# Attention's q and k loads written a component at a time, delta-rule loads counted later, new order weights

## The chip, the cores and the metric

The kernel is one launch on one core of a Trainium2 chip. The metric is device time in microseconds (us), the median of several runs. Five engines work on the core, each through its own stream of instructions in order: TensorE (PE), VectorE (DVE), ScalarE (ACT), GpSimd (POOL) and SyncE (SP). SP computes nothing. It issues the transfers between memory (DRAM) and the on-chip buffers, which have 128 partitions, and 16 DMA engines carry them out.

## What is computed

One layer over 1024 latent tokens and 256 context tokens, 1024 wide, in float32. A combined projection feeds two branches: a bidirectional gated delta rule (8 heads, a scan over chunks) and differential attention (8 heads, two softmaxes of 64 dimensions each per head). Both are normalised, gated, projected, merged and mapped by an output projection. Cut to what matters here:

```python
t = rms_norm(raw.reshape(b, length, DIFF_HEADS, 2, DIFF_DQK), gain)   # q and k: 8 heads, 2 components of 64
...
s = jnp.einsum('bqhcd,bkhcd->bhcqk', qi, k).astype(jnp.float32) * scale
p = jax.nn.softmax(s, axis=-1)
attn = p[:, :, 0] - lam * p[:, :, 1]
return jnp.einsum('bhqk,bkhv->bqhv', attn.astype(v.dtype), v)
...
s_next = s * jnp.exp(gl_i)[..., None, None] + jnp.einsum('bhck,bhcv->bhkv', kd_i, v_new)
```

## The kernel before, in words

Float32 products are made from rounded high parts and low remainders. For a product of weights and activations that means three matmuls in place of one. In attention's scores the two halves of the partitions hold the high and the low part of k, and the matmul sums over both; q's high part `qh` stands in both halves, and q's low part `ql` likewise.

The program runs in stages: front and convolution; the projections of attention's q, k and v; the delta rule; attention; merge and output. The delta rule's scans (`scan`, one for each direction) go head by head over ten chunks, and PE's pauses between their steps are filled with the projections' matmuls (`mm`, out of `fill_flow`). At a change of head, `sets` loads the head's v, k (twice) and q (`vv`, `kk`, `sk`, `sq`), and `loads` loads one pair of chunks at a time (`x`).

Attention (`scores`, `soft`, `turns`, `att_out` and others) goes through 64 tiles: 8 heads of 8 tiles, 128 queries each. A tile takes 12 score matmuls (`s`, two components, three pieces of keys, `qh` then `ql`), an evacuation on DVE, the exponential on ACT, ten transposes (`t`) and, for two tiles together, 30 matmuls with v (`v`). The merge's matmuls (`ma`, from weights `wq` and values `y`) fill PE between them.

`att_load_ops(h)` loads `qh` and `kk` of head h, four transfers. `att_low_ops(h)` loads `ql`, two transfers. Two heads' tiles are held at a time, so the loads of head h wait for the last score of head h-2 (`seen_`). Before, each transfer fills 64 partitions: 64 lines of the 128 of a component-by-dimension array are read in an order that puts component 0 and component 1 of a dimension beside each other. The tiles `vh` and `vl` of v (`att_values`) and the gate `sz` (`gates_in`) have one buffer, and are loaded when the head before has finished with them.

All of attention's loads go through SP's one queue, in the order that the planner wrote down. That order of all engines is made before the chip sees anything. Each stream of work yields steps with an engine, an assumed duration and what they depend on; the planner keeps a clock for each engine and always takes the step that can start first (`flow` in the delta rule, `turn_flow` elsewhere, where steps within `TOL` of one another go by their stream's bias). `ABIAS` holds attention's biases; a stream's bias grows with the tile it works on (`due`). `later(t, us)` makes a result count as ready that much later in the planner's clock. It changes the order alone and puts no wait into the program.

Of the kernel before, what the change touches and what calls it, by code (L numbers as in the profile page):

```python
# [8 lines left out]
F32 = mybir.dt.float32  # L9
# [11 lines left out]
L = 1024  # L21
# [13 lines left out]
PE, DVE, ACT, POOL, DMA, ADMA, DV2, PL1 = range(8)  # L35
# [8 lines left out]
class Block:  # L44
# [193 lines left out]
    def front(self, st, early, kv0):  # L238
# [190 lines left out]
        for g, b in ((loads(), 0), (modulation(), 1), (smalls(), 1), (rms(), 2), (weights(), 1.5), (turns(), 1), (self.forever(turnq[0]), 1.2),  # L429
                     (self.forever(turnq[1]), 1.2), (main(), 9)):  # L430
            self.stream(g, b)
# [822 lines left out]
    def sets(self):  # L1254

        nc = self.nc
        free = []
        for h in range(H):
            yield lambda: self.gs and min(self.scanned) >= h and self.tailed >= h - 1
            w = dict(seen={}, oa=self.gs.tile([P, NL, P], F32, tag=f"oa{h % 2}", name="oa"))  # L1260
            free = [self.over, self.ready[h - 1]["tail"] if h else None]
            for n, src in (("vv", self.gv[h]), ("kk", self.gkk[h]), ("sk", self.gkq[h][:, :LT]), ("sq", self.gkq[h][:, LT:])):
                if h == 0 and n == "kk":
                    yield lambda: all((d, 0, 8) in self.units_ for d in range(2))
                w[n] = self.gs.tile([P, L] if n == "sq" else [P, NT, P] if n in ("kk", "vv") else [P, LT], F32, tag=n, name=n)
                w["t" + n] = yield DMA, 1.82, free, lambda: nc.sync.dma_start(
                    w[n], src.rearrange("(c p) f -> p c f", p=P) if n in ("kk", "vv") else src)
            self.ready[h] = w

    def loads(self, d):  # L1270

        nc, i = self.nc, 0
        order = ((8, 0, 2, 4, 6), (8, 6, 4, 2, 0))[d]
        for h in range(H):
            for c in order:
                yield lambda: self.gs and self.stored > h and len(self.used_[d]) > i - 2
                x, e = self.gs.tile([P, 2, 2, P], F32, tag=f"x{d}", name="x", bufs=2), 2 if c < NL else 1
                u = dict(x=x[:, 0], qk=x[:, 1])
                u["tx"] = yield DMA, 0.45 * e, [self.store_t[h], self.used_[d][i - 2] if i > 1 else None], \
                    lambda: nc.sync.dma_start(x[:, :e], self.xq[h][:, d, c // 2, :e])  # L1280
                if c < NL:
                    u["tqk"] = yield POOL, 0.72, [self.later(u["tx"], 1.0)], lambda: nc.gpsimd.tensor_tensor(
                        x[:, 1], x[:, 1], (self.up, self.lo)[d].unsqueeze(1).to_broadcast([P, 2, P]), ALU.mult)
                self.units_[d, h, c] = u
                i += 1
# [145 lines left out]
    def named(self, n, gen):  # L1431
        s = self.entry[n] = [gen, self.ABIAS.get(n, 0), None, None]
        s[2] = next(gen, None)
        self.streams.append(s)

    def due(self, n, i):

        self.entry[n][1] = self.ABIAS.get(n, 0) + self.DUE * i

# [48 lines left out]
    def att_load_ops(self, h):  # L1488

        q, pool, tags = self.nc.sync, self.a0 if h % 2 else self.gh[0], ("qh", "kk") if h % 2 else ("kq", "X")  # L1490
        w = self.aT[h] = dict(qh=pool.tile([P, 2, L], F32R, tag=tags[0], name="qh"),
                              kk=pool.tile([P, 2, LT], F32R, tag=tags[1], name="kk"))
        old = self.seen_.get(h - 2)
        w["t"] = []
        for s in range(2):
            d, v = slice(64 * s, 64 * s + 64), lambda x: x.rearrange("(c d) n -> d c n", c=2)
            w["t"] += [(yield DMA, 1.46, [old], lambda: q.dma_start(w["qh"][d].bitcast(F32), v(self.qd[0, h]))),
                       (yield DMA, 1.82, [old], lambda: q.dma_start(w["kk"][d].bitcast(F32), v(self.kd[s, h])))]

    def att_low_ops(self, h):  # L1500

        w = self.aT[h]
        w["ql"] = self.a0.tile([P, 2, L], F32R, tag=f"ql{h % 2}", name="ql")
        w["tl"] = []
        for s in range(2):
            w["tl"].append((yield DMA, 1.46, [self.seen_.get(h - 2)], lambda: self.nc.sync.dma_start(
                w["ql"][64 * s:64 * s + 64].bitcast(F32), self.qd[1, h].rearrange("(c d) n -> d c n", c=2))))

    def att_heads(self):
        for h in range(H):  # L1510
# [219 lines left out]
    def side_start(self):  # L1730
# [10 lines left out]
    ONACT = (1, 2, 3)  # L1741
    TOL = 0.02
    PACE = 4.48
    ABIAS = dict(rels=-0.59, softs=8.84, norms=5.82, gateq=-27.29, sums=-14.54,
                 outs=-42.85, lows=-2.4, highs=-9.33, adds=26.02, scales=31.0, evs=22.29, mouts=-3.31,
                 att_out=8.18, turns=3.19, scores=-12.11, merge=1.0)
    KEEP = 3

    def side_values(self):
# [453 lines left out]
```

## Time and profile before

| what | us |
|---|---|
| median of three runs (1963.87 to 1965.93) | 1964.13 |
| the profiled execution, its own time | 1966.57 |
| its span, first to last instruction | 1964.8 |
| PE busy in the span | 1909.4 |
| first score matmul of attention | 1297.4 |
| first score matmul of head 7 | 1720.3 |

The profile's page gives busy time by engine, 40 slices of the span, DMA queues, the chain of work that ended last, and groups of instructions. Other answers of the trace give one tile's instructions, who waited for whom, an engine's instructions in order of time, and busy time, DMA share and rate in chosen stretches. A DMA share of 1 means that all 16 DMA engines were busy; a little over 1 comes from packets that overlap. The PE column counts matmul ends that are modelled, so a full PE is not necessarily at its peak.

### The profile page before, as it was taken

The page shows a single profiled execution, that of the slowest core. Times are in us where ns is not written, and L with a number is a line of the kernel's source. Part 1 is how long each engine was busy: PE and PEld are TensorE (multiplying, and loading weights), DVE is VectorE, ACT ScalarE, POOL GpSimd, SP SyncE. Part 2 cuts the span into 40 slices and gives each one's busy share as a digit, 9 for nine tenths or more (in the row PEclk, how much of TensorE's full clock was granted, in tenths as well). Part 3 has the DMA queues.
Part 4 walks back from the last instruction along what each step waited for, and adds up shares of the span by engine and source line. Part 5 has one row for each costly group of instructions (what it writes and reads, how often), then busy time and mean ns, then how long its engine had stood idle before and what let it go on. Part 6 is the DMA issues. An engine that isn't in the chain of part 4 may idle for free.

```text
span 1964.8 us, 37491 instructions
## 1 busy us (share of the span) xinstructions
PE 1909.4 (97%) x13807; PEld 1679.4 (85%) x13807; DVE 1465.1 (75%) x3613; ACT 1069.4 (54%) x2191; POOL 677.4 (34%) x610
## 2 busy tenths in 40 slices
PE   6999999999999999999999999999999999999999
PEld 4988888899999998888888888877888888888887
DVE  4687998948877987778777673336688979895677
ACT  4543445335325464767755745456687868884222
POOL 3200000005431332343433234233666757762203
PEclk9999999999999999999999999999999999999999
DMA  9144544674546557866777466585566684426542
GB/s 329 60 132 107 144 94 114 145 220 140 183 132 211 150 191 207 257 208 211 249 217 248 114 221 214 153 202 159 159 161 151 156 230 132 129 87 209 182 155 86
DMA packets 383038, 336.39 MB, mean 171 GB/s; under 512 B 142609, under 2 KB 323443, under 8 KB 381831
## 3 DMA queue, kind: packets, MB, share of 16 engines
q1 hardware_dynamic: 382855, 333.99, 57.4%
q8 instruction: 109, 1.79, 0.4%
q14 instruction: 74, 0.61, 0.1%
HBM read 222.14 MB, written 111.79 MB: 170 GB/s over the span
## 4 chain that ended last, share of the span: by engine, by line
PE 77%; DVE 8%; DMA 7%; ACT 3%; issue 2%; SPq 1%; POOL 1%; DVEq 0%; ACTq 0%; POOLq 0%
PE mm L56 38%; PE s L56 6%; PE v L56 6%; PE chain L56 5%; PE mb L56 5%; PE ma L56 4%; PE x L56 3%; PE t L63 3%; PE out L56 2%; DVE S L1560 1%; PE gram L56 1%; DMA vv<-gv 1%; DVE ac L595 1%; PE pz L56 1%; DMA g<-gt 1%
## 5 line engine op out<-in xcount | busy, mean ns | idle before, releaser
L56 PE MATMUL mm<-hs,wh 128*128 128x512 f32 (+1 forms) x2048 | 648.2, 390 | 1.5 <-DVE hs L408 1.4
L56 PEld LDWEIGHTS mm<-hs,wh 128*128 128x128 f32 x2048 | 371.9, 190 | 60.8 <-issue 2.7
L56 PE MATMUL mm<-hs,wl 128*128 128x512 f32 (+1 forms) x1024 | 398.4, 389 | 1.1 <-issue 1.1
L56 PE MATMUL mm<-wh,hs 128*128 128x256 f32 (+1 forms) x1792 | 332.7, 286 | 0.3 <-ACT sq L977 0.3
L56 PEld LDWEIGHTS mm<-wh,hs 128*128 128x128 f32 x1792 | 280.7, 191 | 0.8 <-ACT sq L977 0.5
L1560 DVE TENSOR_SCALAR_CACHE_REDUCE S<-s,rsq 128x512 f32<-128x512 f32 (+1 forms) x384 | 241.4, 656 | 29.4 <-PE s L56 25.9
L56 PE MATMUL mm<-wl,hs 128*128 128x256 f32 (+1 forms) x896 | 255.6, 285 | 0.0
L56 PEld LDWEIGHTS mm<-hs,wl 128*128 128x128 f32 x1024 | 194.4, 190 | 28.7 <-issue 0.9
L1597 POOL TENSOR_TENSOR S<-S 128x1280 f32<-128x1280 f32 x64 | 188.6, 2954 | 78.0 <-ACT S L1590 77.1
L1573 ACT ACTIVATE S<-S,mn 128x1280 f32<-128x1280 f32 x128 | 175.3, 1371 | 44.9 <-DVE mn L1572 43.2
L56 PEld LDWEIGHTS mm<-wl,hs 128*128 128x128 f32 x896 | 171.3, 191 | 0.1
L595 DVE SCALAR_TENSOR_TENSOR ac<-xc,convT,ac 128x1284 f32<-128x1284 f32 (+1 forms) x96 | 138.8, 1449 | 11.9 <-ACT ac L593 11.2
L56 PE MATMUL s<-kk,qh 128*128 128x512 f32 (+1 forms) x384 | 144.5, 376 | 2.9 <-DVE S L1560 2.9
L56 PE MATMUL s<-kk,ql 128*128 128x512 f32 (+1 forms) x384 | 134.0, 359 | 2.5 <-DMA ql<-qd 2.5
L1634 DVE TENSOR_TENSOR al<-t,ah 128x512 fp32r<-128x512 f32 (+1 forms) x192 | 109.5, 596 | 29.8 <-ACT ah L1629 28.9
L1629 ACT CAST ah<-t 128x512 fp32r<-128x512 f32 (+1 forms) x192 | 91.9, 518 | 32.6 <-PE t L63 15.3
L580 POOL MEMSET xc<- 128x2 f32 (+1 forms) x64 | 3.6, 101 | 297.8 <-ACT sq L629 113.6
L63 PE MATMUL t<-ct,S 128*128 128x128 f32 x640 | 98.6, 277 | 4.1 <-DVE al L1634 2.6
L1157 DVE TENSOR_TENSOR ts<-ts,tmp 80x31 f32<-80x31 f32 (+15 forms) x248 | 97.5, 393 | 6.1
L1318 ACT ACTIVATE vd<-chain,edk 128x128 f32<-128x128 f32 x144 | 52.3, 370 | 89.2 <-PE chain L56 83.7
L1155 DVE TENSOR_TENSOR tmp<-ab,ts 80x31 f32<-80x31 f32 (+15 forms) x248 | 94.5, 381 | 8.5 <-DMA ab<-da 3.0
L56 PE MATMUL v<-ah,vh 128*128 128x256 f32 x320 | 93.0, 291 | 0.0
(296 smaller groups left out, 4338.3 us busy)
## 6 DMA issues: line engine op xcount, KB each, us to landing
wr<-in_w_in_dram SPq DMA_DIRECT2D x48, 512.0 KB, 6.0
hx<-in_w_in_dram SPq DMA_DIRECT2D x64, 256.0 KB, 6.4
x<-xq SPq DMA_DIRECT2D x64, 256.0 KB, 3.8
X<-gcd SPq DMA_DIRECT2D x8, 1280.0 KB, 8.3
kd<-col SPq DMA_DIRECT2D x40, 256.0 KB, 2.2
xq<-X SPq DMA_DIRECT2D x16, 640.0 KB, 7.4
kk<-kd SPq DMA_DIRECT2D x16, 640.0 KB, 7.9
kq<-gkq SPq DMA_DIRECT2D x8, 1152.0 KB
```

The lines of the kernel that those rows point to most:

```text
L56: self.nc.tensor.matmul(out, lhsT, rhs, start=start, stop=stop)
L63: self.nc.tensor.transpose(out, src, self.ident[:src.shape[0], :src.shape[0]])
L580: x["e"].append((yield PL1, 0.1, [old], lambda: nc.gpsimd.memset(xc[:, a:b], 0.0)))
L595: t = yield DV2, 1.21e-3 * wd, [t], lambda: nc.vector.scalar_tensor_tensor(ac[:, :wd], xc[:, j:j + wd], self.convw(j, x["ct"]), ac[:, :wd] ...
L1155: t = yield DV2, n * w / 960.0 + 0.08, [t if j else self.later(t, 2.5), t1], lambda: V.tensor_tensor(tv, ab[:, j + 1:, j:j + 1].to_broadca ...
L1157: t = yield DV2, n * w / 960.0 + 0.08, [t, t1], lambda: V.tensor_tensor(ts[:, j + 1:, :w], ts[:, j + 1:, :w], tv, ALU.subtract)
L1318: td = yield ACT, 0.251, [t], lambda: nc.scalar.activation(vd, pc[:, 1], AF.Copy, scale=self.edk[:, c, g:g + 1])
L1560: e = yield DVE, 0.675 if m == 512 else 0.408, [e, self.sfree[c].get(n - 4 + c)], lambda: self.nc.vector.tensor_scalar(x["S"][c][:, o:o + ...
L1573: x["x"].append((yield ACT, 1.36, [e], lambda: nc.scalar.activation(S, S, AF.Exp, bias=x["mn"][:, c:c + 1], scale=-1.0, accum_out=w["l0"][ ...
L1597: e = yield POOL, 2.9, [e], lambda: self.nc.gpsimd.tensor_tensor(S0, S0, S1, ALU.add)
L1629: e = yield ACT, 0.48 if nb == 4 else 0.27, [t, y["old", k]], lambda: self.nc.scalar.copy(y["ah", k][:, :, q], pv)
L1634: t = yield DVE, 0.603 if k < 2 else 0.322, [e, y["old", k]], lambda: self.nc.vector.tensor_tensor(y["al", k][:, :, q], pv, y["ah", k][:, ...
```

## The change

Each of the six loads of a head fills one component of all 128 partitions now, and not both components of 64. For q the source is the component's 64 lines, read twice by a leading step of two that does not move; for k the leading step of two goes from the high part's array to the low part's. The bytes of each transfer are the same (512 KB for `qh` and `ql`, 640 KB for `kk`), and so are the tiles.

In the delta rule, the results of `sets`' loads count as ready 1.3 us later, and those of `loads` 1.0 us later for every user, where before only the POOL step that masks them counted so. Six of attention's biases have new values.

```diff
@@ sets, loads
                 w["t" + n] = yield DMA, 1.82, free, lambda: nc.sync.dma_start(
                     w[n], src.rearrange("(c p) f -> p c f", p=P) if n in ("kk", "vv") else src)
+                w["t" + n] = self.later(w["t" + n], 1.3)
...
+                u["tx"] = self.later(u["tx"], 1.0)
                 if c < NL:
-                    u["tqk"] = yield POOL, 0.72, [self.later(u["tx"], 1.0)], lambda: nc.gpsimd.tensor_tensor(
+                    u["tqk"] = yield POOL, 0.72, [u["tx"]], lambda: nc.gpsimd.tensor_tensor(
@@ att_load_ops
-        for s in range(2):
-            d, v = slice(64 * s, 64 * s + 64), lambda x: x.rearrange("(c d) n -> d c n", c=2)
-            w["t"] += [(yield DMA, 1.46, [old], lambda: q.dma_start(w["qh"][d].bitcast(F32), v(self.qd[0, h]))),
-                       (yield DMA, 1.82, [old], lambda: q.dma_start(w["kk"][d].bitcast(F32), v(self.kd[s, h])))]
+        for c in range(2):
+            d = slice(64 * c, 64 * c + 64)
+            w["t"] += [(yield DMA, 1.46, [old], lambda: q.dma_start(
+                           w["qh"][:, c].bitcast(F32), self.qd[0, h, d].unsqueeze(0).to_broadcast([2, 64, L]))),
+                       (yield DMA, 1.82, [old], lambda: q.dma_start(w["kk"][:, c].bitcast(F32), self.kd[:, h, d]))]
@@ att_low_ops
-        for s in range(2):
+        for c in range(2):
             w["tl"].append((yield DMA, 1.46, [self.seen_.get(h - 2)], lambda: self.nc.sync.dma_start(
-                w["ql"][64 * s:64 * s + 64].bitcast(F32), self.qd[1, h].rearrange("(c d) n -> d c n", c=2))))
+                w["ql"][:, c].bitcast(F32), self.qd[1, h, 64 * c:64 * c + 64].unsqueeze(0).to_broadcast([2, 64, L]))))
@@ ABIAS
-    ABIAS = dict(rels=-0.59, softs=8.84, norms=5.82, gateq=-27.29, sums=-14.54,
-                 outs=-42.85, lows=-2.4, highs=-9.33, adds=26.02, scales=31.0, evs=22.29, mouts=-3.31,
-                 att_out=8.18, turns=3.19, scores=-12.11, merge=1.0)
+    ABIAS = dict(rels=-0.59, softs=8.84, norms=5.82, gateq=-27.29, sums=-18.71,
+                 outs=-21.73, lows=-2.4, highs=-9.33, adds=36.19, scales=31.0, evs=22.29, mouts=-3.31,
+                 att_out=1.9, turns=3.19, scores=-21.22, merge=25.46)
```

Since every later step of the planner follows from the earlier ones, the order differs from the first change of head on, on all engines. Three places matter below. The first is SP's queue at the end of the delta rule, where head 0's `qh` and `kk` are loaded. (`hx<-in_w_in_dram` are the filling projections' weights, `x<-xq` the scan's pairs of chunks, `hx<-sza` and `ya` belong to the delta rule's output.) Before:

```order
L1404 DMA ya<-sz 128x512
L1405 DMA ya<-oa 128x512
L1497 DMA qh<-qd 64x2x1024
L1498 DMA kk<-kd 64x2x1280
L1497 DMA qh<-qd 64x2x1024
L1498 DMA kk<-kd 64x2x1280
L1371 DMA hx<-sza 128x1024
L1280 DMA x<-xq 128x512
L880 DMA hx<-in_w_in_dram 128x4x128
L1280 DMA x<-xq 128x512
L1038 DMA gt<-zo 128x1024
L880 DMA hx<-in_w_in_dram 128x4x128
```

The same place now:

```order
L1281 DMA x<-xq 128x512 x2
L1407 DMA ya<-oa 128x512
L1499 DMA qh<-qd 128x1x1024
L1501 DMA kk<-kd 128x1x1280
L1499 DMA qh<-qd 128x1x1024
L1501 DMA kk<-kd 128x1x1280
L1373 DMA hx<-sza 128x1024
L880 DMA hx<-in_w_in_dram 128x4x128 x2
L1038 DMA gt<-zo 128x1024
L880 DMA hx<-in_w_in_dram 128x4x128 x2
```

The last of the scan's loads now stand ahead of head 0's q and k, and the projections' weights stand directly behind them, as before.

The second is SP's queue in attention, behind the loads of head 2. The rows are head 1's v and gate (`vh`, `vl`, `sz`), the merge's weights (`wq`) and its gate (`g`). Before, from `vh` on:

```order
L1525 DMA vh<-vd 128x4x128
L1525 DMA vl<-vd 128x4x128
L1767 DMA wq<-in_w_oa_dram 128x4x128
L1525 DMA vh<-vd 128x4x128
L1525 DMA vl<-vd 128x4x128
L1525 DMA vh<-vd 128x2x128
L1525 DMA vl<-vd 128x2x128
L1767 DMA wq<-in_w_oa_dram 128x4x128
L1698 DMA sz<-szb 128x1024
```

The same now, with the last of head 2's loads ahead:

```order
L1509 DMA ql<-qd 128x1x1024 x2
L1770 DMA wq<-in_w_oa_dram 128x4x128 x2
L1794 DMA g<-gt 128x512
L1528 DMA vh<-vd 128x4x128
L1528 DMA vl<-vd 128x4x128
L1770 DMA wq<-in_w_oa_dram 128x4x128 x2
L1528 DMA vh<-vd 128x4x128
L1528 DMA vl<-vd 128x4x128
L1528 DMA vh<-vd 128x2x128
L1528 DMA vl<-vd 128x2x128
L1701 DMA sz<-szb 128x1024
```

In both, a head's v and gate are issued after the next head's q and k; the merge's loads around them have moved.

The third is PE at a change of head in the delta rule, to head 5: `chain<-vv,x` is the first step of each direction's scan, `mm` the filling. Before:

```order
L56 MATMUL chain<-vv,x 128x128
L56 MATMUL mm<-hs,wh 128x512 x2
L56 MATMUL mm<-hs,wl 128x512
L56 MATMUL mm<-hs,wh 128x512 x2
L56 MATMUL chain<-vd,kk 128x128
L56 MATMUL chain<-vv,x 128x128
```

Now:

```order
L56 MATMUL mm<-hs,wl 128x512
L56 MATMUL mm<-hs,wh 128x512 x2
L56 MATMUL chain<-vv,x 128x128
L56 MATMUL mm<-hs,wl 128x512
L56 MATMUL mm<-hs,wh 128x512 x2
L56 MATMUL mm<-hs,wl 128x512
L56 MATMUL chain<-vv,x 128x128
```

Some three matmuls of filling stand between the two first steps in both; what stands ahead of the first one differs by what the later count let in.

## Prediction, made before the changed kernel had run

> **What bounds the kernel now.** I read the page first: busy time by engine, then DMA queues and issues.
>
> ```profile
> span 1964.8 us, 37491 instructions
> PE 1909.4 (97%) x13807; PEld 1679.4 (85%) x13807; DVE 1465.1 (75%) x3613; ACT 1069.4 (54%) x2191; POOL 677.4 (34%) x610
> q1 hardware_dynamic: 382855, 333.99, 57.4%
> kk<-kd SPq DMA_DIRECT2D x16, 640.0 KB, 7.9
> qh<-qd SPq DMA_DIRECT2D x16, 512.0 KB, 9.3
> ql<-qd SPq DMA_DIRECT2D x16, 512.0 KB, 15.4
> hx<-in_w_in_dram SPq DMA_DIRECT2D x64, 256.0 KB, 6.4
> ```
>
> PE is idle for 55.4 us in the whole span, so that is all a better hidden load could return. The DMA engines are busy for 57% of the span: room for faster transfers, and for slower ones up to a point. The 48 loads that change land 8 to 15 us after their issue.
>
> Next, who waited for whom on PE: the delta rule's second part (640 to 1297 us), then attention (1297 to 1795).
>
> ```profile
> PE chain L56 <- DMA vv<-gv: 2.2, 4, 1.1
> PE chain L56 <- DMA x<-xq: 1.8, 1, 1.8
> PE chain L56 <- DMA sk<-gkq: 1.6, 1, 1.6
> PE chain L56 <- DMA kk<-gkk: 0.7, 2, 0.5
> PE s L56 <- DMA ql<-qd: 2.5, 1, 2.5
> PE s L56 <- DVE S L1560: 2.9, 6, 1.9
> ```
>
> Columns: total us, times, longest. The head changes' loads cost 6.3 us in all, attention's loads 2.5 us, once, less than its waits for the evacuation of scores on DVE (last row). Loads are hidden almost everywhere.
>
> Third, how fast loads go, from busy time in chosen stretches. The columns behind POOL are granted clock, DMA share and GB/s.
>
> ```profile
> 1352.00:1358.00 6.00, 6.00 (x39) 5.46 (x39) 5.03 (x19) 3.49 (x6) 0.00 (x0) 0.96 1.05 408
> 1373.00:1384.00 11.00, 10.30 (x58) 8.65 (x58) 6.51 (x23) 6.26 (x13) 7.22 (x4) 1.00 1.03 208
> 1345.00:1500.00 155.00, 148.46 (x948) 131.20 (x947) 123.86 (x412) 115.44 (x196) 94.83 (x49) 0.98 0.62 166
> 1500.00:1650.00 150.00, 147.41 (x953) 129.85 (x952) 130.90 (x446) 116.62 (x198) 98.48 (x52) 1.00 0.68 179
> 1650.00:1795.00 145.00, 142.07 (x925) 124.30 (x924) 122.47 (x388) 113.47 (x189) 90.62 (x44) 1.00 0.44 128
> ```
>
> In the first stretch `y<-ya` loads write 128 partitions: all engines full, 408 GB/s, 25.5 GB/s from each of 16. In the second head 2's q and k loads write 64 partitions: engines just as full, 208 GB/s. So the old loads do hold each engine twice as long as loads over 128 partitions. The last three rows are attention: PE idle for 12.1 of 450 us (155 - 148.46, 150 - 147.41, 145 - 142.07).
>
> **The change, part by part.** A head's six loads move 2 x (512 + 640 + 512) KB = 3.41 MB. Before, that takes 3.41 / 208 GB/s = 16.4 us.
>
> *On how many engines.* The new loads write 128 partitions, but their source begins with a step of two, and inside it come the 64 lines. No row of this trace shows a large load whose source begins with fewer than 32 steps: `x`, `y`, `wq`, `v` begin with 128, the old q and k with 64 on both sides. So the price is bounded. If all 16 engines share, it is 3.41 / 408 = 8.4 us a head. If each step of the leading two goes to one engine, it is 3.41 MB / (2 x 25.5 GB/s) = 67 us. The nearest row is a small one:
>
> ```profile
> rows<-in_c_dram SPq DMA_DIRECT2D x1, 4.0 KB
> ```
>
> It begins with eight steps, and the trace's completion signals (in no view; counted from its records) tell it apart. A signal shared by 124 loads that all have a multiple of 16 steps came 1984 times, 16 for each. One shared by 123 such and this load came 1977 times: 123 x 16 and 9. Another, with three loads of eight steps among 124, came 1963 times: 121 x 16 and 3 x 9. So eight steps do not run on 16 engines here; the leading count sets how many take part. I take two engines, 67 us a head, and keep 8.4 us as the other end.
>
> The Trainium skill, "DMA: Bandwidth & Descriptors" (Why a DMA increments its semaphore by 16 and not by 1; Rules for kernel authors), says that the engine count is the largest number up to 16 that divides the outermost counts of both sides, and that a leading broadcast of c copies confines a DMA to c engines, the lowest-numbered; by it the sum is the one below. The counted signals agree with it for eight steps; no run here shows two.
>
> *Head 0's first loads.* SP's queue in order of time:
>
> ```profile
> 1225.96 0.61 SPq L1498 DMA_DIRECT2D kk<-kd  x1
> 1231.23 0.39 SPq L880 DMA_DIRECT2D hx<-in_w_in_dram  x1
> 1290.89 1.23 SPq L1506 DMA_DIRECT2D ql<-qd  x2
> 1302.95 0.60 SPq L1498 DMA_DIRECT2D kk<-kd  x1
> 1367.46 0.59 SPq L1497 DMA_DIRECT2D qh<-qd  x1
> 1436.47 0.59 SPq L1497 DMA_DIRECT2D qh<-qd  x1
> 1489.60 0.59 SPq L1497 DMA_DIRECT2D qh<-qd  x1
> ```
>
> The four loads of `qh` and `kk` (2.36 MB) now hold two engines for 2.36 / 51 = 46 us. The projections' weights are issued some 5 us behind the last of them, and since every load has its share on those two engines too, they come when the 46 us are over. The chain of work that ended last has this load already:
>
> ```profile
> 1231.23 12.63 DMA hx<-in_w_in_dram
> ```
>
> So there is no slack: 46 + 6.4 us from 1226 is 1278, against 1244 before. PE's filling stops, and the scan behind it in PE's order: +30 us, a little under the difference. Then the two `ql` take 1.05 MB / 51 = 21 us where 8.7 was measured for one: +12. The first score goes from 1297 to about 1340.
>
> *Heads 1 to 7.* Head 1's loads follow at once (1303 before, so about 1343 now), and land 67 + 3 us later, at 1413, the 3 us for head 0's v in front (1.31 MB / 408 GB/s). From there each head is a ring:
> - head h+1's loads: 67 us;
> - head h's v and gate, issued behind them and so landing behind them: 1.31 + 0.52 MB at 408 GB/s, 4.5 us;
> - the last two tiles of head h, which stand in PE's order behind head h's first product with v, and whose end frees the buffers of head h+2: 2 x 6.6 = 13 us, with a tile from the issues above, (1489.60 - 1436.47) / 8;
> - half of the other traffic, which SP issues in front (`wq`, `g`, `ma`, `rr`, `yb`: some 3.2 MB a head, 8 us): 4 us.
>
> That is 88 us for a head, where the issues above are 69 and 53 us apart. Once, 4.2 MB of `y` add 10 us. Head 7's loads land at 1413 + 6 x 88 + 10 = 1951. From its first score to the end nothing changes:
>
> ```profile
> 1720.31 0.40 PE L56 MATMUL s<-kk,qh 128*128 128x512 f32 x1
> ```
>
> 1964.8 - 1720.3 = 244.5 us, so the end is at 2195.5. The profiled execution took 1966.57, 0.1% above the median of 1964.13, so no correction is needed between them: **2195 us**.
>
> *Later counts and new weights.* The 6.3 us of head-change waits are the most that the later counts can return; at worst each of 8 heads starts its scan 1.3 + 1.0 us later, 18 us. Filling covers this: PE lacks only 15.2 us in these 657 us.
>
> ```profile
> 640.00:1000.00 360.00, 350.52 (x3342) 316.12 (x3343) 292.39 (x821) 224.04 (x624) 128.24 (x151) 1.00 0.68 214
> 1000.00:1297.00 297.00, 291.28 (x2418) 251.41 (x2418) 164.71 (x452) 159.57 (x462) 97.16 (x126) 0.99 0.62 188
> ```
>
> The new weights can return at most attention's 12.1 us and may lose as much. I take zero for both; in the forecast case PE waits for loads anyway and neither shows.
>
> **The rivals.**
>
> *All engines share the new loads* (or each load gets another pair, six side by side: 0.66 MB / 51 = 13 us for the longest). Place: the same 48 loads; they land sooner than now, and 2.5 us plus part of 6.3 us come back, some 6 us: 1958, range 1945 to 1972. For it: the destination has 128 partitions, and the row at 408 GB/s shows what such a destination takes. Against it: the counted signals. It decides from four engines on: 3.41 / (4 x 25.5) = 33 us and the ring's other 21 us fit into the 53 us between two issues. This is the case that ends at not slower.
>
> *The order alone loses.* Loads as fast as in the first rival, but the later counts let filling go ahead of the scan and the scan ends later: 18 us at most, some 10: 1975. For it: DVE and ACT work of the same heads waits with the scan. Against it: the three filling matmuls between the first steps have not become more.
>
> *Two engines, but little of the ring is exposed:* v, gate, tiles and other traffic all pass beside the loads. Then 67 us a head alone: 1413 + 6 x 67 + 244.5 = 2060. Against it: v's place behind the loads in SP's queue. The other way, an engine may give only its mean over the program, 333.99 MB over 57.4% of 16 x 1964.8 us, 18.5 GB/s: 92 us of loads and 113 a head, 2370.
>
> **How the numbers follow.** Forecast (two engines, the ring) 0.83, all engines 0.13, the order alone 0.04. Within the forecast the ends 2060 and 2370 are each unlikely; 2090 to 2310 leaves out some 0.03 of its 0.83 and the other cases, so it holds 0.80. A difference under 0.2% (4 us) can't be told from none. Faster: 0.09 from the second case. Same: 0.02 from it. Slower: 0.83, 0.02 from it (weights that lose) and 0.04, 0.89.
>
> **What would show it.** Two engines: in attention the share falls below 0.3 while q and k load, with a rate near 51 GB/s; the scores wait for `ql` or `kk` tens of us, seven times; issues of `qh` stand 80 to 95 us apart; the filling stops for some 30 us behind head 0's loads, and PE's granted clock dips behind such pauses. Head times near 67 would say that the ring is hidden, above 100 that two engines give less than 51 GB/s. If instead q and k land within 8 us at a share near 1, the step from leading count to engines was wrong, and with it the forecast.

## The result, and the profile after

| kernel | median, us | runs | ratio to before | 95% interval |
|---|---|---|---|---|
| before, same chips | 1965.03 (1963.87 to 1967.3) | 4 | | |
| changed | 2320.40 (2320.16 to 2321.8) | 4 | 1.1808 | 1.1788 to 1.1829 |

The changed kernel is 355 us slower. The forecast was 2195 with 2090 to 2310 about it: the direction and the number of engines were right, but the time lies 125 us above it, just outside the range.

The page of the changed kernel, its head, the slices of the granted clock and of the DMA engines, SP's DMA queue, and the chain that ended last:

```profile
span 2318.4 us, 37465 instructions
PE 1919.4 (83%) x13807; PEld 1689.1 (73%) x13807; DVE 1456.4 (63%) x3613; ACT 1067.6 (46%) x2191; POOL 679.3 (29%) x610
...
PEclk9999999999999999999999686787869687889999
DMA  7344456654646777758654224131241323124652
...
q1 hardware_dynamic: 382183, 333.99, 46.0%
...
PE 61%; SPq 18%; DMA 10%; DVE 5%; ACT 2%; issue 2%; POOL 1%; DVEq 0%; ACTq 0%; POOLq 0%
```

PE is idle for 2318.4 - 1919.4 = 399.0 us, 343.6 more than before, and its matmuls take 10.0 us longer, since the granted clock falls behind the pauses (the slices with 6 to 8). Together that is the 353.6 us by which the span grew. The same 333.99 MB keep the DMA engines busy for a smaller part of a longer span. In attention's slices the share falls to 0.1 to 0.4. `SPq` has 18% of the chain, against 1% before: time in which the chain runs through SP's own issuing of transfers. The planner counts 0.5 us of SP for an issue (`SPI` in the kernel) and no more.

Whom PE waited for (total us, times, longest):

```profile
PE v L56 <- DMA vh<-vd: 117.0, 3, 40.2
PE v L56 <- ACT ah L1632: 50.4, 1, 50.4
PE ma L56 <- DVE g L1809: 49.0, 2, 48.0
PE m L63 <- POOL bry L179: 45.8, 1, 45.8
PE t L63 <- DVE mn L1575: 42.1, 1, 42.1
PE out L56 <- ACT vn L1324: 37.4, 1, 37.4
PE s L56 <- DMA ql<-qd: 18.1, 1, 18.1
```

These are nine pauses, 358.7 us in sum: 37.4 in the filling, 18.1 for head 0's `ql`, and one of 38.0 to 50.4 in each of seven heads. None of the seven names `qh`, `kk` or `ql`. Five different tiles are named. In the chain that ended last, each of the seven goes back to a transfer that SP issued behind those loads. Three are `vh`; the other four (start of the issue, us until the chain goes on) are:

```profile
1413.42 19.31 DMA gt<-zo
1497.12 25.07 DMA wq<-in_w_oa_dram
1705.39 15.63 DMA g<-gt
1910.91 26.39 DMA rr<-rbd
```

`gt<-zo` is a store for which ACT's `ah` waited, `rr` a load for which POOL waited. So what PE lacks is whatever stood behind the q and k loads. In the kernel before, the medians from issue to landing were 3.3 us for `wq` and 3.7 for `g`: being issued did not end the delay. That their share on the two engines lay behind the loads there would explain it, and no run tests it.

One head in stretches (columns as in the prediction: length, busy time of PE, PEld, DVE, ACT, POOL, granted clock, DMA share, GB/s), from the issue of head 2's loads to that of head 3's:

```profile
1452.00:1465.00 13.00, 12.75 (x84) 11.32 (x84) 11.99 (x43) 12.12 (x21) 7.25 (x4) 1.00 0.11 43
1465.00:1497.00 32.00, 9.22 (x62) 8.00 (x60) 6.22 (x22) 4.40 (x9) 5.98 (x3) 0.70 0.13 52
1497.00:1520.00 23.00, 0.00 (x0) 0.00 (x0) 0.00 (x0) 0.00 (x0) 0.00 (x0) 0.50 0.23 80
1520.00:1557.00 37.00, 31.61 (x198) 27.93 (x199) 28.53 (x99) 28.57 (x47) 25.88 (x15) 0.88 0.37 112
```

A share of 0.13 is two engines of 16, at 52 GB/s. Counted from the trace's packet records, exactly two packets of these loads' sizes were under way for 64.6 of the 67.5 us in which any was. PE works for 22 us, then PE, DVE, ACT and POOL all stand still, then 32 us of work follow. The rule of the Trainium skill, "DMA: Bandwidth & Descriptors" (Rules for kernel authors), that the prediction cited, a leading broadcast of c copies on at most c engines, agrees with that row.

SP's queue in order of time over the same head (start, us that SP spent on it, instruction; x2 is two issues):

```profile
1452.29 0.51 SPq L1499 DMA_DIRECT2D qh<-qd  x1
1452.90 0.48 SPq L1501 DMA_DIRECT2D kk<-kd  x1
1453.44 8.09 SPq L1499 DMA_DIRECT2D qh<-qd  x1
1461.58 12.28 SPq L1501 DMA_DIRECT2D kk<-kd  x1
1473.90 23.11 SPq L1509 DMA_DIRECT2D ql<-qd  x2
1497.12 15.14 SPq L1770 DMA_DIRECT2D wq<-in_w_oa_dram  x2
1512.32 5.76 SPq L1794 DMA_DIRECT2D g<-gt  x1
1527.88 0.37 SPq L1528 DMA_DIRECT2D vh<-vd  x1
...
1558.07 0.53 SPq L1499 DMA_DIRECT2D qh<-qd  x1
```

An issue that took 0.6 us before takes 8 to 12 us from the third load on, and `wq` and `g` behind them are slow as well, though they have 128 steps. SP gets on about as fast as the two engines work off such loads (10 us for 512 KB and 13 for 640 KB at 51 GB/s, an estimate). The four loads from the third on, two `wq` and one `g` take it 65 us; `vh` comes 76 us behind the first `qh`, the last 10 of them waiting for PE's matmuls with the `vh` before.

And the step from there to PE, ACT in order of time (in brackets the idle time before an instruction and its releaser):

```profile
1468.32 1.33 ACT L1632 CAST ah<-t 128x512 fp32r<-128x512 f32 x3
1522.21 0.62 ACT L1779 CAST wh<-wq 128x512 fp32r<-128x512 f32 x1 [52.56 <-DMA wq<-in_w_oa_dram]
...
1524.00 1.33 ACT L1632 CAST ah<-t 128x512 fp32r<-128x512 f32 x3
```

ACT takes its work in order: at 1469.6 it comes to the rounding of a merge weight, and stands for 52.6 us in front of the exponentials and `ah`, which PE's next matmul needs. This is the pause of 50.4 us.

### The profile page after: what moved, and what is told of

It reads as the page before. It is cut to its first block, busy times and chain, and to the rows that moved or that the text cites. A ratio compares the mean times of both kernels' runs of the same rounds, so it can differ in the third digit from the quotient of the medians.

```text
span 2318.4 us, 37465 instructions
## 1 busy us (share of the span) xinstructions
PE 1919.4 (83%) x13807; PEld 1689.1 (73%) x13807; DVE 1456.4 (63%) x3613; ACT 1067.6 (46%) x2191; POOL 679.3 (29%) x610
## 3 DMA queue, kind: packets, MB, share of 16 engines
q1 hardware_dynamic: 382183, 333.99, 46.0%
## 4 chain that ended last, share of the span: by engine, by line
PE 61%; SPq 18%; DMA 10%; DVE 5%; ACT 2%; issue 2%; POOL 1%; DVEq 0%; ACTq 0%; POOLq 0%
PE mm L56 34%; SPq L1509 7%; SPq L1501 4%; PE chain L56 4%; PE mb L56 4%; SPq L1499 3%; PE s L56 3%; PE x L56 3%; PE v L56 3%; DMA vh<-vd 3%; PE out L56 2%; PE ma L56 2%; PE t L63 1%; DMA rr<-rbd 1%; DMA wq<-in_w_oa_dram 1%
## 5 line engine op out<-in xcount | busy, mean ns | idle before, releaser
L56 PEld LDWEIGHTS v<-ah,vh 128*128 128x128 f32 x320 | 63.5, 198 | 171.3 <-issue 118.0
L56 PE MATMUL s<-kk,ql 128*128 128x512 f32 (+1 forms) x384 | 136.5, 367 | 18.1 <-DMA ql<-qd 18.1
L56 PE MATMUL ma<-y,wh 128*128 128x512 f32 x256 | 95.4, 419 | 49.0 <-DVE g L1809 49.0
L63 PE MATMUL t<-ct,S 128*128 128x128 f32 x640 | 87.0, 273 | 46.6 <-DVE mn L1575 42.1
L63 PEld LDWEIGHTS t<-ct,S 128*128 128x128 f32 x640 | 74.1, 140 | 54.8 <-issue 45.3
L1595 POOL TENSOR_TENSOR S<-S,rl 128x1280 f32<-128x1280 f32 x16 | 37.2, 2325 | 214.9 <-DVE rl L1586 121.5
```

The source lines that it names most:

```text
L56: self.nc.tensor.matmul(out, lhsT, rhs, start=start, stop=stop)
L63: self.nc.tensor.transpose(out, src, self.ident[:src.shape[0], :src.shape[0]])
L1595: e = yield POOL, 2.4, [e], lambda: nc.gpsimd.tensor_tensor(S, S, rl.to_broadcast([P, LT]), ALU.mult)
```

## The experiments

**The changed kernel's parts.** Four kernels separate the form of the loads from the order. The first keeps all of the change and turns the two source dimensions round, so that the 64 lines lead and the step of two lies inside:

```diff
-                           w["qh"][:, c].bitcast(F32), self.qd[0, h, d].unsqueeze(0).to_broadcast([2, 64, L]))),
-                       (yield DMA, 1.82, [old], lambda: q.dma_start(w["kk"][:, c].bitcast(F32), self.kd[:, h, d]))]
+                           w["qh"][:, c].bitcast(F32), self.qd[0, h, d].unsqueeze(1).to_broadcast([64, 2, L]))),
+                       (yield DMA, 1.82, [old], lambda: q.dma_start(w["kk"][:, c].bitcast(F32), self.kd[:, h, d].rearrange("s d n -> d s n")))]
...
-                w["ql"][:, c].bitcast(F32), self.qd[1, h, 64 * c:64 * c + 64].unsqueeze(0).to_broadcast([2, 64, L]))))
+                w["ql"][:, c].bitcast(F32), self.qd[1, h, 64 * c:64 * c + 64].unsqueeze(1).to_broadcast([64, 2, L]))))
```

> The changed kernel with one difference: in each q and k load the 64 dimensions lead and the pair (q twice; k's high and low part) comes inside, so that a partition holds the other order of the same numbers, in q and k alike. Bytes, destination partitions and the order of every engine are those of the changed kernel. If the leading count of two puts a load on two DMA engines (the changed kernel: 2320.4 us), the loads now run on 16: a head's six loads take about 8.4 us (3.41 MB at the 408 GB/s of the kernel before), PE's nine pauses of 18 to 50 us go, and the time is 1945 to 1972 us. If the 128-partition destination or the new order is what costs, it stays above 2250 us.

Measured: 1943.79 us (4 runs), ratio 0.9893 to before, 0.9875 to 0.9911, a little under the expected range. Head 2's loads, from their issue at 1403.7 on:

```profile
1404.00:1414.00 10.00, 10.00 (x67) 8.81 (x66) 8.94 (x31) 9.15 (x16) 5.16 (x2) 1.00 1.00 389
```

All 16 engines, 389 GB/s, and PE no longer waits for any of attention's loads (the only loads that its waits name are the front's `wa` and the delta rule's `sk` and `vv`). Bytes, tiles, partitions and the order of all engines are those of the changed kernel: the leading count alone makes 2320.4 - 1943.8 = 377 us. This kernel is also faster than both.

The second keeps the change's counts and weights and takes the loads of the kernel before (the lines with a minus in the diff of the change); the third is the kernel before with the change's loads alone (the lines with a plus); the fourth is the kernel before with the loads of the first.

> The changed kernel with the loads of before (64 partitions each), but with the later counts and the new weights. If the loads alone made the loss, 1950 to 1980 us; the difference from before is what counts and weights are worth (forecast: between -18 and +18 us, zero taken). If the new order makes PE depend on late transfers, above 2100 us. Beside the run with the dimensions leading, it also tells what 128 partitions are worth in the same order: at most the 2.5 us that scores waited for a load before.

> The kernel before with nothing but the new loads (leading count two); counts, weights and so the order are those of before. If the loads alone made the loss: 2250 to 2400 us, with pauses of PE once a head. If the order's interplay with them made most of it: under 2150 us.

> The kernel before with nothing but loads over 128 partitions whose 64 dimensions lead. If 16 engines carry them, a head's loads take half of the 16.4 us of before and at most the 2.5 us of waiting for them come back: 1958 to 1966 us. If faster loads get in the way of the others, 1970 us or more.

| order, counts, weights | old loads | two lead | 64 lead |
|---|---|---|---|
| of before | 1965.25 (9 runs) | 2328.86 (1 run) | 1956.60 (5), 0.9959 (0.9943 to 0.9975) |
| of the change | 1951.65 (5), 0.9937 (0.9924 to 0.995) | 2320.40 (4) | 1943.79 (4) |

Read across: the change's loads cost 363.6 and 368.8 us in the two orders, and over 128 partitions on all engines they gain 8.7 and 7.9. Read down: the later counts and new weights gain 13.6, 8.5 (one of the two times is a single run) and 12.8 us. The gain from 128 partitions on all engines is more than the 2.5 us that were expected at most: with it PE works 455.01 us between 1297 and 1760 us of the old order, 5.7 more than before, so more came back than the one wait that names a load. A packet of `kk` (5120 bytes) took a median of 413 ns before, 200 ns in the changed kernel and 196 ns in the first of these (counted from the packet records): writing 128 partitions does halve an engine's time for a packet; it was the number of engines that was lost.

**How the pause grows with the loads.** In the changed kernel `qh` and `kk` are loaded as before, or `kk` alone (below); the other loads keep the leading two:

```diff
-            d = slice(64 * c, 64 * c + 64)
+            d, v = slice(64 * c, 64 * c + 64), lambda x: x.rearrange("(c d) n -> d c n", c=2)
...
-                       (yield DMA, 1.82, [old], lambda: q.dma_start(w["kk"][:, c].bitcast(F32), self.kd[:, h, d]))]
+                       (yield DMA, 1.82, [old], lambda: q.dma_start(w["kk"][d].bitcast(F32), v(self.kd[c, h])))]
```

> The changed kernel with qh and kk loaded 64 partitions at a time as before, and only the two ql of a head with the leading count of two. On two engines these two (1.05 MB) take 20.5 us a head, the other four about 12 us on 16 engines beside them. Theory A (everything behind the head's loads in SP's queue waits for them, PE goes on for about 25 us with what it has, and stops for the rest): a pause of 5 to 15 us a head and 12 us at head 0, 2000 to 2060. Theory B (loads cost nothing as long as they fit into the 53 to 56 us between two heads' issues): only head 0's 12 us and little else, 1955 to 1970. SP's own issue: if it stops because two such loads are already queued, both ql are issued in about 0.5 us each, since there are only two at a time.

> The changed kernel with kk alone loaded 64 partitions at a time; qh and ql with the leading count of two: 2.1 MB on two engines, 41 us a head. Theory A (PE goes on for about 25 us and stops for the rest): a pause of about 20 us a head, 2080 to 2160. My predicted ring with 41 in place of 67 us of loads: 62 us a head, 2010 to 2050. Theory B (hidden because 41 us fit into the 53 to 56 us between issues): under 1980.

Measured: 2045.75 and 2175.23 (one run each). The first is where theory A had it, the second 15 us above; theory B and the predicted ring (2010 to 2050 for the second) fell. From PE's matmuls in each trace, the seven pauses behind the loads of heads 1 to 7, and the issues of `qh` that follow one another:

| kernel | two engines busy with a head's loads, us | mean of seven pauses | busy minus pause | between issues of `qh` |
|---|---|---|---|---|
| `ql` alone | 20.5 + 11.3 = 31.8 | 9.1 | 22.7 | 68.8 |
| `ql` and `qh` | 41.0 + 6.3 = 47.3 | 25.9 | 21.4 | 85.2 |
| all (the change) | 67.0 | 43.3 | 23.7 | 102.8 |
| none (old loads) | | 0 | | 57.1 |

(The second terms are the old loads on all engines: 2.36 and 1.31 MB at the prediction's 208 GB/s.) So, on the mean of seven heads, work covers 21 to 24 us of the loads' time, and every further microsecond is a pause. (In single heads of the changed kernel it is 17 to 29 us, 67.0 less pauses of 50.4 to 38.0.) That loads would be hidden up to the 53 to 56 us between two issues fell: 32 us already cost 94 us against the old loads, 18 of them PE's wait for head 0's `ql`.

SP's queue with `ql` alone on two engines:

```profile
1388.18 3.73 SPq L1508 DMA_DIRECT2D ql<-qd  x2
1392.00 18.63 SPq L1769 DMA_DIRECT2D wq<-in_w_oa_dram  x2
```

The two `ql` were to go in 0.5 us each and took 3.7 together; then the two `wq` behind them, over all engines, take 18.6. SP gets about two such loads ahead and no further.

**Which wait it is.** The merge's weights are loaded once and kept, so that ACT never waits for them; 15 of 16 of these loads are left out, so the output is another.

```diff
+            if kept:
+                for s in range(2):
+                    t = yield DMA, 0.73, [free[s]], lambda: None
+                    kept[s] = kept[s][0], t
+                return list(kept)
...
-                rs.append((r, (yield DMA, 0.73, [free[s]], lambda: nc.sync.dma_start(r, src[:, 4 * s:4 * s + 4]))))
+                kept.append((r, (yield DMA, 0.73, [free[s]], lambda: nc.sync.dma_start(r, src[:, 4 * s:4 * s + 4]))))
```

> The changed kernel with the merge's weights wq loaded for the first block alone and used for all blocks (15 of 16 loads left out, the output is another; order and arithmetic the same). ACT then never stops at the merge's weights (147.8 us in three waits in the changed kernel). Theory A1 (ACT's stop at wq is what ends PE's supply early in those heads): PE runs on longer before each such pause, rings 10 to 15 us shorter on three heads or more, 2270 to 2300. Theory A2 (v and the gates stand behind the same loads and stop PE at nearly the same time): the pauses stay and are put down to other tiles, 2305 to 2320.

Measured: 2299.05 (one run), at the upper end of A1. Whom PE waited for:

```profile
PE v L56 <- DMA vh<-vd: 115.4, 3, 38.7
...
PE m L63 <- DVE mn L1575: 36.6, 1, 36.6
```

Of the seven, only the pause that had named ACT's `ah` became shorter by more than 2 us, from 50.4 to 36.6, and went to the next transfer in line (`g`, for which DVE then stood 36.5 us). A1 asked for three such heads or more: it holds for one, and A2 for the other six.

**The place in the queue.** The six loads of a head are issued by POOL in place of SP, with the same leading counts:

```diff
-        q, pool, tags = self.nc.sync, self.a0 if h % 2 else self.gh[0], ("qh", "kk") if h % 2 else ("kq", "X")
+        q, pool, tags = self.nc.gpsimd, self.a0 if h % 2 else self.gh[0], ("qh", "kk") if h % 2 else ("kq", "X")
...
-            w["tl"].append((yield DMA, 1.46, [self.seen_.get(h - 2)], lambda: self.nc.sync.dma_start(
+            w["tl"].append((yield DMA, 1.46, [self.seen_.get(h - 2)], lambda: self.nc.gpsimd.dma_start(
```

> The changed kernel with the six loads of a head issued by POOL in place of SP, at the same places of the planner's order; bytes and leading counts the same, so two engines carry 67 us of them a head. Theory A (it is their place in SP's one queue, and the time for which SP stops at issuing them, that holds back v, the gates and wq): these no longer wait for the q and k loads, a head takes 67 us of loads and little else, 2080 to 2220; POOL stops at the issues in SP's place, and its own work (sums over partitions, the gates' products) is late. Theory C (the two engines' own rings are what v and the gates wait in, whatever the queue, since a part of each of those loads runs on the same two engines): as the changed kernel, 2280 to 2340.

Measured: 1986.67 (one run), where neither theory had it. KB of each load and us from issue to landing:

```profile
kk<-kd POOLq DMA_DIRECT2D x16, 640.0 KB, 25.9
...
ql<-qd POOLq DMA_DIRECT2D x16, 512.0 KB, 27.3
```

In the packet records of POOL's queue 7 to 8 packets of these loads are under way on the mean of each of heads 2 to 7, for long stretches 10 to 13, and a head's loads are over in 27 to 33 us, not 67. A load of 512 KB alone on two engines would take 0.52 MB / 51 GB/s = 10 us; six side by side on different pairs would use 12 engines. That is the "another pair" of the prediction's first rival, though on a queue it did not think of. The same page of the Trainium skill (Why a DMA increments its semaphore by 16 and not by 1) states that a transfer issued by POOL on fewer than 16 engines takes the next ones in turn, while SP's always take the lowest-numbered; the 10 to 13 packets here and the 2 in the changed kernel agree in number, though the records do not name the engine. A row of the same page of the Trainium skill (Rules for kernel authors) says that spreading DMAs over SP, ACT and GpSimd doesn't help bandwidth, since all run on the same 16 engines. For loads that take only two of them, the choice of the queue did matter here: 27 to 33 us against 67. So this run did not tell the two theories apart, because the loads no longer shared two engines.

The other way round, then: q and k loads stay on SP with two leading, and `v`, `wq` and `g` go to POOL; a control does the same to the kernel with the old loads.

```diff
-                    t = yield DMA, 0.73, [self.vfree[k]], lambda: self.nc.sync.dma_start(
+                    t = yield DMA, 0.73, [self.vfree[k]], lambda: self.nc.gpsimd.dma_start(
...
-                rs.append((r, (yield DMA, 0.73, [free[s]], lambda: nc.sync.dma_start(r, src[:, 4 * s:4 * s + 4]))))
+                rs.append((r, (yield DMA, 0.73, [free[s]], lambda: nc.gpsimd.dma_start(r, src[:, 4 * s:4 * s + 4]))))
...
-            tg = yield DMA, 0.73, self.gfree_[:1], lambda: self.nc.sync.dma_start(gt, self.gt[m][:, o * 512:o * 512 + 512])
+            tg = yield DMA, 0.73, self.gfree_[:1], lambda: self.nc.gpsimd.dma_start(gt, self.gt[m][:, o * 512:o * 512 + 512])
```

> The changed kernel, its q and k loads still issued by SP with the leading count of two, but v, wq and g of attention (some 4 MB a head) issued by POOL, at the same places of the planner's order. If what stops PE is their place behind the q and k loads in SP's queue, they now land beside them: ACT and DVE no longer stop at wq and g, a head takes the 67 to 70 us of its loads and little else, and the 43 us of pause a head fall to 10 to 15: 2060 to 2130. If what stops PE is that a sixteenth of each of these loads waits in the same two engines, the pauses stay: 2290 to 2330. POOL's own work (27 to 35 us of a head) is later by the time of some 16 issues in both.

> The control to the kernel before it in this set: v, wq and g issued by POOL in the same way, q and k loaded 64 partitions at a time as before, with the later counts and new weights. What POOL's issues cost by themselves: against 1951.65 without them, 1955 to 1990.

Measured: 2336.86 and 1967.36 (one run each): no gain at all, and a time that only the second of the two theories comes near. But its reason is not what happened: the transfers themselves, issued beside the q and k loads, landed soon (first fence), and the pauses went elsewhere (second, waits of PE, DVE and POOL):

```profile
wq<-in_w_oa_dram POOLq DMA_DIRECT2D x32, 256.0 KB, 6.4
vh<-vd POOLq DMA_DIRECT2D x16, 256.0 KB, 7.7
```

```profile
PE v L56 <- DVE oT L1674: 154.5, 4, 39.7
PE m L63 <- POOL bry L179: 112.2, 4, 56.5
...
DVE oT L1674 <- DMA sz<-szb: 158.0, 4, 40.2
...
POOL oT L1723 <- DMA rr<-rbd: 113.4, 2, 58.0
```

The medians of 6.4 and 7.7 us are above the 3.3 and 5.4 of the kernel before: the two engines cost these transfers a few us, SP's queue cost them tens. The time stayed since transfers still on SP came in their place. In four heads it is the gate `sz`: PE waits for `v`'s evacuation `oT` on DVE, and DVE for `sz`. In two it is `rr`, for which POOL stands before it makes `bry`, and at head 0 it is `gt`. So the rest of the heads' transfers went to POOL too (`sz`, `rbd`, `rr`, `yb`, `ma`, by the same edit in their lines). That leaves SP the q and k loads, `y`, and `gt` at head 0. PE's, DVE's and ACT's order is untouched.

> The changed kernel, its q and k loads on SP with the leading count of two, and all other transfers of attention's heads (v, wq, g, sz, rbd, rr, yb, ma) issued by POOL; PE's, DVE's and ACT's order unchanged. If the place in SP's queue is what makes the pauses, nothing is left behind the q and k loads: a head takes the 67 to 70 us of its loads and little else, 13 to 17 us of pause instead of 43, and 18 us at head 0: 2060 to 2130, PE's pauses put down to ql or kk. If another wait takes their place again (POOL stops in its own order at rr or ma and is late with the sums): 2150 to 2250, the pauses put down to POOL. If the two engines hold up everything whatever the queue: 2300 or more.

> The control to it: the same transfers issued by POOL, q and k loaded 64 partitions at a time as before on SP, later counts and new weights kept. With v, wq and g alone on POOL it was 1967.36; five more kinds, some of them stores that wait for DVE: 1965 to 2000.

Measured: 2224.64 and 1969.45 (one run each). That is 95.8 us below the changed kernel, and more than the hoped 2060 to 2130. It lies where a wait for POOL was to put it, but the pauses are not put down to POOL. PE's largest waits, and SP's queue over a head:

```profile
PE s L56 <- DMA ql<-qd: 101.8, 6, 22.2
PE t L63 <- DVE mn L1575: 44.1, 1, 44.1
PE out L56 <- ACT vn L1324: 36.4, 1, 36.4
PE ma L56 <- DMA y<-ya: 29.4, 1, 29.4
```

```profile
1516.50 11.08 SPq L1499 DMA_DIRECT2D qh<-qd  x1
...
1559.93 32.19 SPq L1509 DMA_DIRECT2D ql<-qd  x2
1593.18 9.05 SPq L1499 DMA_DIRECT2D qh<-qd  x1
```

Now the scores wait for `ql`, as the prediction had thought, and in the heads shown SP issues one head's loads directly behind the last's. A head takes 83.0 us (issues of `qh` from 1455.9 to 1870.8, five heads). Two waits are not of this kind: 44.1 us at head 0 and 29.4 us for `y`, whose transfers (`gt` and `y`) still stood on SP. So what stood behind the loads on SP's queue is worth 96 us of the 369 that the leading count of two costs in this order, by one run; POOL's issues cost 18 of themselves (the control against 1951.65), so it may be some 18 more. Of the 255 us that stay against the control, PE's waits for `ql` make 102, the filling's stop 36 and the two other waits 74.

Why the two engines need 83 us in place of 67 for a head, the packet records answer: they have POOL's transfers to carry as well. Between 1457.5 and 1950 us, six heads, POOL's packets fill 100 us of each of the 16 engines on the mean, 16.7 us a head. Fewer than two packets of the q and k loads were under way for 135 us of that time, and POOL's were for 87 to 88% of these 135 us, against 24% while there were two. The records do not name the engine, so this is a strong sign and not a test.

**Counts and weights.** Each alone in the kernel before (edits as in the diff of the change), five rounds:

> The kernel before with the later counts of the delta rule's loads alone; attention's loads and weights as before. With the weights they are worth -13.6 us. The head changes' waits for loads are 6.3 us in the kernel before: if the counts remove those waits and no more, 1958.5 to 1962 (-3 to -6.5). If the counts carry most of the 13.6, 1952 to 1956, and then the gain lies in the scans' length, not in those waits. If the weights carry all of it, 1964 to 1967.

> The kernel before with attention's new weights alone. The counts alone made no difference (0.9997). If the gain of 13.6 us is the weights' own, 1949 to 1954; PE is idle for 12.1 of the 450 us of attention in the kernel before, so a gain above that must come partly from the merge behind attention. If counts and weights gain only together, 1960 to 1966.

Measured: 1962.95 (12 runs), ratio 0.9997 (0.9983 to 1.0012), and 1963.99 (12 runs), ratio 0.9995 (0.9983 to 1.0008). Neither alone does anything that can be told from none; together they gave 0.9937, the case that the second text names last. Busy time in chosen stretches, of one profile each, hints at why. Attention in the kernel before; then the delta rule's first stretch and attention in the kernel with the counts alone; then attention with counts and weights and the old loads:

```profile
1297.00:1760.00 463.00, 449.35 (x2820) 393.47 (x2819) 373.64 (x1261) 350.80 (x578) 286.97 (x144) 0.99 0.59 157
```

```profile
640.00:1000.00 360.00, 358.54 (x3386) 324.77 (x3385) 286.63 (x810) 215.77 (x615) 131.02 (x152) 1.00 0.69 219
...
1297.00:1760.00 463.00, 442.73 (x2791) 383.17 (x2790) 376.59 (x1279) 353.41 (x580) 288.85 (x144) 1.00 0.58 157
```

```profile
1297.00:1760.00 463.00, 450.70 (x2856) 394.72 (x2856) 380.59 (x1291) 360.08 (x593) 295.71 (x146) 0.99 0.59 158
```

The counts give PE 8.0 us more work in the delta rule (358.54 against the prediction's row of 350.52), and attention, with an order that follows from another start, gives back 6.6 (442.73 against 449.35). The new weights bring attention to 450.70 in that order. But alone, in the old order, they bring it to 453.07 and gain no time, so these stretches don't account for the whole. That the weights fit this order better than the old one is argued, not shown.

## Why the prediction was right or wrong

**Number of engines: right.** The counted signals of one small load were the only evidence from a trace, and 0.13 of the engines at 52 GB/s is what the prediction took. Its other ends fell: all engines sharing is a time of 1956.60 in the old order, but only where 64 leads. Its rival said 1958, in part by luck, since it took only named waits back and PE gained 5.7 us in attention's stretch, where 2.5 were named. And 18.5 GB/s to an engine is refuted by the same 52 GB/s. Leading counts between 2 and 64 were not tried, so that four engines would have been enough is open.

**Head 0: right in place, small by some 18 us.** The filling stopped for 37.4 us where 30 were taken; the first score came at 1339.1. That this met the 1340 is luck: the forecast had `ql`'s 12 us in it, and PE waited 18.1 us more behind that score.

**The ring: the step that failed.** Against its own numbers, first scores and the tail:

| | predicted | measured | difference |
|---|---|---|---|
| first score of head 1 | 1413 | 1453.9 | +41 |
| from there to head 7 | 6 x 88 + 10 = 538 | 613.9 | +76 |
| from there to the end | 244.5 | 250.6 | +6 |

That is all of the 123 us between 2195.5 and the span; 18.1 of the first 41 are head 0's wait for `ql`. The terms for the transfers were nearly right: 67 + 4.5 + 4 = 75.5 us from a head's first issue to the end of what waits for it, where the quoted head has 1524.6 - 1452.3 = 72.3 to PE's next matmul, and all seven have 71 to 77. The term that failed is "the last two tiles of head h", 13 us: it took for granted that PE, DVE and ACT do the rest of head h under the loads, some 44 of 57 us. From the first issue to the pause PE worked for 22 to 35 us, 30 on the mean. After the pause 33.5 us of the quoted head (1524.6 to 1558.1), and 29 on the mean of six (18 to 47), were left to do before head h+2's loads could be issued. The mean of 74 up to PE's next matmul and these 29 make the 103 us measured between two issues of `qh`, against 88. The prediction had `wq`, `g`, `ma`, `rr` and `yb` in front of the loads and priced them by their bytes; what counts is that some stand behind, that SP can't issue them meanwhile, and that ACT and DVE, in order, stop at the first that is missing, whoever needs it. In three of the seven heads the wait is for `vh`, as the term had it, and 21 us were left behind it in the two that are followed by another head's loads. In the other four an engine in front of PE stopped first, and 18 to 47 us were left.

**SP's time: not in the prediction.** It read SP's issues at 0.6 us each and took it that SP never stops, that only the transfers wait for one another. Taking the heads' other transfers off SP won 96 us, which is SP's slow issues and the place behind the loads together; no run parts the two.

**What would show it.** Share and rate, the filling's stop and the clock's dips came as listed. The waits for `ql` or `kk`, seven times, did not: `ql` once, and other tiles seven times. The reading set beside issues more than 100 us apart, that two engines would give less than 51 GB/s, was wrong: they stood 102.8 us apart at 52 GB/s.

**Counts and weights at zero: wrong by 8.5 us here, 13.6 without the slow loads.** The 6.3 us were no bound on the idle time that the counts could return, since they took only PE's waits that name a load: in the delta rule's first stretch alone it shrank by 8.0, though the counts by themselves gained nothing over the whole.

## What to carry to other kernels

Before a load is rewritten for more partitions, look at the outermost count of its source as well as of its destination: here the same bytes over the same partitions cost 369 us against the old loads with two outermost and gained 8 with 64. A slow load is priced by what stands behind it on its queue and by the first such item that each in-order engine runs into, not by who reads the load; the useful numbers are how long the engines go on without the queue (30 us on the mean here) and how much of the round is left when it moves again (29). Weights of an order and another edit that gain together may gain nothing alone, as here.

## What was not expected of the hardware

- SP's issue of a transfer, 0.6 us otherwise, took 8 to 12 us once some two loads of 64 packets for each of the two engines were ahead of it, and 6 to 19 us (for one `g`, for two `wq`) for transfers over all engines behind them.
- Issued by POOL, loads of the same form ran 10 to 13 packets wide for long stretches, and a head's were over in 27 to 33 us in place of 67; an issue took POOL some 0.8 us.
- Beside two engines that were full with SP's loads, transfers of POOL's that use all engines still landed in 6.4 and 7.7 us (medians of `wq` and `vh`; 3.3 and 5.4 in the kernel before).
